# Two-layer hybrid encoder on one core: the start, the splitting of weights, two product ends and the last residual rewritten

## The chip, the core and the metric

The kernel runs on one core of a Trainium2 chip. The time is device microseconds of one execution; lower is better. The engines are TensorE (PE; its weight loads are listed apart as PEld), VectorE (DVE), ScalarE (ACT), GpSimd (POOL), and SyncE (SP), which here issues nearly all DMA transfers.

## The reference, cut to what matters

```python
for l in range(2):                      # x is (1, 1024, 1024), all float32
    z = rmsnorm(x, g_pre_mix[l]) @ w_in[l]            # 1024 -> 256 | 512 | 128 | 128 | 256
    zf, zq, zk, zv, zm = split(z)
    y_f = real(fft2 over (sequence, 64 channels) of zf) @ w_fourier[l]   # 4 groups
    y_a = window attention (|i-j| <= 128, 8 q heads, 2 kv heads, RoPE, sink)
    km, vm = split(rmsnorm(mem, g_mem[l]) @ w_mem_kv[l])    # 256 memory rows, 256 + 256 columns
    y_m = softmax(zm @ km^T / 8) @ vm                       # 4 heads
    y = concat(rmsnorm of y_f, y_a, y_m, with g_grp[l]) @ w_out[l]
    x = x + rmsnorm(y, g_post_mix[l])
    gate, up = split(rmsnorm(x, g_pre_ffn[l]) @ w_ffn_in[l])     # 2 x 2816
    x = x + rmsnorm((silu(gate) * up) @ w_ffn_out[l], g_post_ffn[l])
return x
```

## The kernel before, in words

**Split products.** Every large matrix product takes its operands as a high part (rounded to float32r) and a low part, what is left over, and adds three matmuls per block: high by high, high by low, low by high. `split` makes the two parts of a block: ACT casts the high part and DVE, or POOL where it is named, subtracts it from the block for the low one. Weights are loaded into a raw buffer first. `raws` is a ring of raw buffers at slots 0, 2 and 4 of the arena `arena_f` (a slot is 256 float32 columns), so three loads can be under way at once. Where a gain belongs to the weights (`g`, one number per weight row), it is multiplied in while the parts are made.

**Weight loads that the change touches.** `load_w` (L372) loads blocks into a raw buffer, has POOL scale them with `scaled` (L369) if there is a gain, and splits them. `zf_load` (L547) uses it for the 256 columns of w_in that give zT, with the low part on POOL. `load_w512` (L391) loads the eight 128x512 blocks of the kvz and q weights: in even blocks ACT writes the scaled high part and DVE makes the low part from the raw block in one instruction (L407); in odd blocks POOL scales the raw block in place, ACT casts and POOL subtracts. `Memory.load_k` loads the key half of w_mem_kv as two times 128 columns.

**The start.** Tiles of x (128 rows each) are loaded by `start_load`, squared and summed on ACT (`token_scale`), transposed on PE into PSUM banks of the pool "pd" and split into hT (`norm_T`). `fourier_tables` loads w_fourier and makes small tables with PE ("abp"). `prep` makes the position tables. `mem.make` loads the memory rows and weights, transposes the rows ("mTp") and makes keys and values ("kmp", "vmp", in "pd" banks as well). `mix.zf(half)` makes zT for four tiles out of hT and the zT weights, 48 matmuls of 512 columns, and then the products "pq" with the Fourier tables. Program order at the start is: tile 0, the pre-mix gains, tiles 1 to 3, the zT weights, tile 4; then the four tiles, the tables, `prep`, the memory, and last tiles 4 to 7 interleaved with `zf(0)`.

**The second feed-forward product.** `ffn_out` forms the 1024x1024 result from seven products of half-size blocks, in the order 5, 3, 4, 1, 7, 2, 6. Each has eleven steps k, and each step three matmuls into each of four PSUM banks p: 132 matmuls named "fo" (L1357). `out_sums` prepares a step: it loads a block of activations and one or two of weights, adds the two weight blocks on DVE (L1338) and splits both. The prepared operands of a step stand in a ring `abs_`, of six places in layer 0 and fifteen in layer 1. Products 3 and 7 go on adding in the PSUM banks of 5 and 1, so a bank has to be read out in between: after product 5 by two ACT copies per bank (L1381, L1382), after product 1 by a DVE addition (L1390). In layer 0 the work for layer 1 is put between: `mem.make` after product 3, `zf_load` and `fourier_tables` after product 1. In layer 1 the last tiles' output follows product 6, whose last two banks are done one after the other.

**The end.** `residual_out` squares and sums f (1024 columns) on ACT, makes 1/rms on POOL (two small instructions), then for each half of 512 columns multiplies f by it and by the gain (L354), adds it to x (L355, on POOL for tiles 1 and 3) and stores the half (L356).

**What sets the order.** The kernel is built with a planner (`schedule_with_timeline_sim=True`): it takes the program order as priorities, simulates a timeline with its own costs and from that writes out one fixed order of instructions for every engine and for SP. On the chip each engine goes through its order and waits where an operand is missing; whatever stands behind the waiting instruction on the same engine waits too. An edit at one place can therefore change the order at others. `tc.issue_after(ins)` holds the instructions of a block behind `ins`.

Of the kernel before, what the change touches and what calls it, by code (L numbers as in the profile page):

```python
# [19 lines left out]
P = 128  # L20
# [49 lines left out]
def tile_encoder(ctx: ExitStack, tc: tile.TileContext, T, C, out):  # L70
# [276 lines left out]
    def residual_out(x, f, g, dst, t):  # L347

        ss = sm(1, "rss")
        nc.scalar.activation(junks(D // 2).bitcast(BF16), f, AF.Square, accum_out=ss)  # L350
        r = rsqrt_mean(ss, D, 1, "rrs")
        for n in range(2):
            ns = slice(n * 512, n * 512 + 512)
            nc.vector.scalar_tensor_tensor(out=f[:, ns], in0=f[:, ns], scalar=r[:, 0:1], in1=g[:, ns], op0=ALU.mult, op1=ALU.mult)  # L354
            (nc.gpsimd if t in (1, 3) else nc.vector).tensor_tensor(out=x[:, ns], in0=x[:, ns], in1=f[:, ns], op=ALU.add)  # L355
            (nc.sync, nc.scalar)[n].dma_start(dst[:, ns], x[:, ns])  # L356
# [33 lines left out]

    def load_w512(w, c0, g):  # L391


        res = []
        for k in range(NK):
            if k % 2 == 0:
                t = big(2, 2, 512)
            raw = raws(512)
            nc.sync.dma_start(raw, w[k * P : k * P + P, c0 : c0 + 512])
            hi, lo = t[:, k % 2, 0], t[:, k % 2, 1]  # L400
            if k % 2:
                scaled(raw, g, k)
                split(hi, lo, raw, nc.gpsimd)
            else:
                gk = g[:, k : k + 1]
                nc.scalar.activation(hi, raw, AF.Copy, scale=gk)
                nc.vector.scalar_tensor_tensor(out=lo, in0=raw, scalar=gk, in1=f32(hi), op0=ALU.mult, op1=ALU.subtract)  # L407
            res.append((hi, lo))
        return res
# [31 lines left out]
    class Memory:  # L441
# [7 lines left out]
        def load_k(self):  # L449
            self.wk = [load_w(self.w, ci * P, P, self.kw + 8 * ci) for ci in range(2)]  # L450

        def load_v(self):
            self.wv = load_w(self.w, MW, MW, self.kw + 16)

        def rows(self):
            self.h = [at(self.kx + 4 + 4 * mt, D) for mt in range(2)]
            for mt in range(2):
                nc.sync.dma_start(self.h[mt], T["mem"][0, mt * P : (mt + 1) * P, :])

        def norm(self, mt):  # L460
            if mt == 0:
                self.g = gain(T["g_mem"][self.l], at(self.kx, D))
                self.mT = [[at(self.kt + 8 * i + 4 * kg, 4, NMEM, dt=F32R) for kg in range(2)] for i in range(2)]
            h = self.h[mt]
            norm_x(h, self.g)
            for kg in range(2):
                pt = ps([4, P], "mTp", "pT")
                for j in range(4):
                    k = kg * 4 + j
                    nc.tensor.transpose(pt[:, j, :], h[:, k * P : (k + 1) * P], ident)  # L470
                sl = slice(mt * P, mt * P + P)
                split(self.mT[0][kg][:, :, sl], self.mT[1][kg][:, :, sl], pt)
# [4 lines left out]
        def keys(self, ci):  # L477
            pt = ps([NMEM], "kmp", self.tag)
            acc = Acc(pt, NK)
            for k in range(NK):  # L480
                acc.add(self.wk[ci][k][0], self.wk[ci][k][1], self.m(0, k), self.m(1, k))
            nc.scalar.activation(at(self.ks + ci, NMEM), pt, AF.Copy, scale=QK_SCALE)
# [9 lines left out]
        def make(self):  # L492
            self.rows()
            self.load_k()
# [25 lines left out]
    class Mix:  # L520
# [26 lines left out]
        def zf_load(self):  # L547
            self.wzf = load_w(self.win, 0, 256, 64, nc.gpsimd, self.g)

# [164 lines left out]
        def kvz_load(self):  # L714

            self.wkvz = load_w512(self.win, FW + AW, self.g)
            self.vst, self.zst, self.kvr = {}, {}, {}
# [44 lines left out]
        def q_load(self):  # L762
            self.wq = load_w512(self.win, FW, self.g)
            self.qst, self.qr = {}, {}
# [577 lines left out]
    def ffn_out(l, actd, load, out, after, half, late):  # L1342
# [16 lines left out]
        for i in (5, 3, 4, 1, 7, 2, 6):  # L1359
# [5 lines left out]
            for k in range(n):  # L1365
                ops.append(out_sums(l, actd, i, k))
                for p in range(whole):
                    step(pts[p], p, ops[k], k == 0, k == n - 1, new)
# [6 lines left out]
            for p in range(4):  # L1375
                pt = pts[p]
                if p >= whole:
                    for k in range(n):
                        step(pt, p, ops[k], k == 0, k == n - 1, new)
                if i == 5:  # L1380
                    nc.scalar.copy(c22[p], pt)  # L1381
                    nc.scalar.copy(c11[p], pt)  # L1382
                if i == 3:
                    nc.scalar.copy(c12[p], pt)
                    TT(out=c22[p], in0=pt, in1=c22[p], op=sub)
                if i == 4:
# [45 lines left out]
    mix = Mix(0, hT, mem)  # L1432
    start_load(0)
    gains_T(gpT, T["g_pre_mix"], at(15, P))
    for t in range(1, 4):
        start_load(t)
    mix.zf_load()
    start_load(4)
# [4 lines left out]
    mem.make()  # L1443
    weave([lambda t=t: start_tile(t) for t in range(4, 8)], [lambda: mix.zf(0)])

    for l in range(DEPTH):
        mix.zf(1, 2)
        mix.kvz_load()
        kvz = mix.skewed(mix.kvz, mix.kvz_turn, NT)
        weave(mix.fourier_units(), kvz[:8] + [mix.q_load] + kvz[8:])  # L1450
# [143 lines left out]
```

## Time and profile before

| | |
|---|---|
| median of 3 runs | 2010.85 us (2010.7 to 2011.73) |
| the profiled execution | 2013.01 us, its span 2011.2 us |
| mean granted clock of PE | 0.995 |
| busy PE, PEld | 1967.6 us (98%), 1628.7 us (81%) |
| busy DVE, ACT, POOL | 1489.6, 1047.6, 657.2 us (74%, 52%, 33%) |
| moved by DMA | 288.56 MB, 143 GB/s over the span |

The rows of the profile name an instruction by the line of the kernel that issues it, often a line of a helper (L176 and L177 are the two lines of `split`), by engine and operation, and by the tiles it writes and reads. In the view of waits a row gives who waited, for whom, how long in sum, how often and the longest. In the order of time a row gives start, duration, instruction and count, and in brackets the idle time before it with what ended it. The granted clock is a share of TensorE's full clock.

### The profile page before, as it was taken

How to read it: one execution, taken by the hardware profiler on the slowest of the kernel's cores; microseconds unless marked ns; L12 is line 12 of the kernel's file. 1: busy time of each engine (PE TensorE's matmuls, PEld its weight loads, DVE VectorE, ACT ScalarE, POOL GpSimd, SP SyncE). 2: the span in 40 equal slices, each digit the busy share in tenths (PEclk: the TensorE clock that was granted, in tenths of full speed). 3: DMA queues.
4: the chain of work that ended last, by engine and by line, in shares of the span. 5: the costliest groups of instructions: out<-in, count | busy, mean ns of one | idle time of the engine just before them, and what ended most of it. 6: DMA issues, size and time to landing. Idle time of an engine off the chain costs nothing.

```text
span 2011.2 us, 28323 instructions
## 1 busy us (share of the span) xinstructions
PE 1967.6 (98%) x9587; PEld 1628.7 (81%) x9587; DVE 1489.6 (74%) x2364; ACT 1047.6 (52%) x2204; POOL 657.2 (33%) x793
## 2 busy tenths in 40 slices
PE   8999999999999999999999999999999999999998
PEld 7877888788888888887888778877888888887886
DVE  5566867888777766678866677679887777778776
ACT  6476877643433334554555678676343333345541
POOL 4345445204334333002423654451134333400021
PEclk9999999999999999999999999999999999999999
DMA  6210323444323224979831113244332332379973
GB/s 214 64 59 27 110 101 127 135 131 136 100 95 121 85 88 157 310 265 322 286 132 45 53 59 116 95 147 126 126 120 95 121 100 95 110 232 330 314 273 116
DMA packets 181889, 288.56 MB, mean 143 GB/s; under 512 B 15560, under 2 KB 81648, under 8 KB 181744
## 3 DMA queue, kind: packets, MB, share of 16 engines
q1 hardware_dynamic: 173680, 267.88, 40.1%
q10 hardware_dynamic: 8064, 18.88, 2.4%
q8 instruction: 75, 1.23, 0.3%
q14 instruction: 70, 0.57, 0.1%
HBM read 220.11 MB, written 66.58 MB: 143 GB/s over the span
## 4 chain that ended last, share of the span: by engine, by line
PE 87%; DVE 3%; DMA 3%; ACT 2%; issue 2%; POOL 2%; SPq 0%; DVEq 0%; POOLq 0%; ACTq 0%
PE fo L1357 18%; PE qy L1193 12%; PE qx L1193 12%; PE qc L1193 11%; PE mo L187 7%; PE qz L1193 6%; PE kvp L187 4%; PE qp L187 4%; PE zT L187 2%; PE sc L793 2%; PE pT L831 2%; PE qa L1193 1%; PE av L844 1%; DMA arena_f<-in_w_ffn_out 1%; DVE arena_r L177 1%
## 5 line engine op out<-in xcount | busy, mean ns | idle before, releaser
L1357 PE MATMUL fo<-arena_r 128*128 128x512 f32 x1512 | 354.6, 391 | 6.6 <-ACT big L1382 4.0
L1357 PEld LDWEIGHTS fo<-arena_r 128*128 128x128 f32 x1512 | 284.0, 188 | 66.2 <-ACT big L1382 4.8
L176 ACT CAST arena_r<-arena_f 128x512 fp32r<-128x512 f32 (+2 forms) x344 | 185.8, 572 | 179.5 <-DMA arena_f<-actd 69.2
L177 DVE TENSOR_TENSOR arena_r<-arena_f,arena_r 128x512 fp32r<-128x512 f32 x262 | 182.3, 727 | 52.0 <-ACT arena_r L176 44.2
L1193 PE MATMUL qc<-arena_r,flex 128*128 128x512 f32 x912 | 220.8, 390 | 0.0
L1183 ACT CAST flex<-arena_f 128x512 fp32r<-128x512 f32 x148 | 91.8, 621 | 232.2 <-PE qy L1193 71.3
L1193 PEld LDWEIGHTS qc<-arena_r,flex 128*128 128x128 f32 x912 | 171.1, 188 | 37.1 <-DVE flex L1125 0.2
L1193 PE MATMUL qy<-arena_r,flex 128*128 128x512 f32 x576 | 139.4, 389 | 0.0
L1183 ACT CAST arena_r<-arena_f 128x512 fp32r<-128x512 f32 x92 | 57.0, 621 | 156.6 <-DVE arena_f L1180 63.7
L1193 PEld LDWEIGHTS qy<-arena_r,flex 128*128 128x128 f32 x576 | 108.0, 188 | 22.6
L1184 DVE TENSOR_TENSOR flex<-arena_f,flex 128x512 fp32r<-128x512 f32 x148 | 108.4, 734 | 22.7 <-ACT flex L1183 22.7
L1227 POOL TENSOR_TENSOR arena_f<-arena_f 128x512 f32<-128x512 f32 x36 | 48.1, 1336 | 231.7 <-ACT arena_f L1198 231.7
L1193 PE MATMUL qx<-arena_r 128*128 128x512 f32 x360 | 119.5, 389 | 0.0
L1193 PE MATMUL qy<-arena_r 128*128 128x512 f32 x480 | 116.4, 389 | 0.0
L1184 DVE TENSOR_TENSOR arena_r<-arena_f,arena_r 128x512 fp32r<-128x512 f32 x92 | 67.7, 736 | 62.6 <-ACT arena_r L1183 60.5
L1193 PE MATMUL qz<-arena_r,flex 128*128 128x512 f32 x320 | 106.8, 395 | 0.0
L1259 POOL TENSOR_TENSOR arena_f<-arena_f,flex 128x512 f32<-128x512 f32 x28 | 45.7, 1632 | 184.9 <-DVE arena_f L1230 114.1
L1193 PEld LDWEIGHTS qy<-arena_r 128*128 128x128 f32 x480 | 90.1, 188 | 18.7
L1234 POOL TENSOR_TENSOR arena_f<-arena_f 128x512 f32<-128x512 f32 x36 | 60.0, 1668 | 126.5 <-DVE arena_f L1233 126.5
L187 PE MATMUL mo<-big,arena_r 128*128 128x512 f32 x384 | 100.4, 398 | 0.5 <-ACT arena_f L1043 0.5
L1193 PE MATMUL qx<-flex,flex 128*128 128x512 f32 x304 | 100.1, 390 | 0.0
L1180 DVE TENSOR_TENSOR arena_f<-arena_f 128x512 f32<-128x512 f32 x90 | 92.5, 1033 | 4.4 <-DMA arena_f<-in_w_ffn_in 2.9
(315 smaller groups left out, 4624.1 us busy)
## 6 DMA issues: line engine op xcount, KB each, us to landing
arena_f<-in_w_ffn_out SPq DMA_DIRECT2D x264, 256.0 KB, 4.7
actd<-arena_f SPq DMA_DIRECT2D x154, 256.0 KB, 3.0
arena_f<-actd SPq DMA_DIRECT2D x154, 256.0 KB, 4.5
arena_f<-in_w_ffn_in SPq DMA_DIRECT2D x46, 512.0 KB, 3.9
big<-in_w_ffn_in SPq DMA_DIRECT2D x40, 512.0 KB, 4.5
arena_f<-in_w_in SPq DMA_DIRECT2D x40, 256.0 KB, 2.9
arena_f<-in_x SPq DMA_DIRECT2D x16, 512.0 KB, 5.3
arena_f<-in_w_out SPq DMA_DIRECT2D x32, 256.0 KB, 2.7
```

The lines of the kernel that those rows point to most:

```text
L176: nc.scalar.copy(hi, src)
L177: return (lo_eng or nc.vector).tensor_tensor(out=lo, in0=src, in1=f32(hi), op=ALU.subtract)
L187: mm(self.dst, a, b, start=self.i == 0, stop=self.i == self.n - 1)
L793: mm(pt, lhs, self.kst[g][i][:, k0 * P : k1 * P], start=i == 0, stop=i == 1)
L1180: nc.vector.tensor_tensor(out=s, in0=x, in1=y, op=op)
L1183: self.cast = nc.scalar.copy(w[:, 0], s)
L1184: self.lo = nc.vector.tensor_tensor(out=w[:, 1], in0=s, in1=f32(w[:, 0]), op=ALU.subtract)
L1193: mm(pt, a, b, start=start and n == 0, stop=n == 11, skip_group_check=not start)
L1227: G(out=self.u2, in0=self.u2, in1=self.p1, op=ALU.add)
L1234: G(out=self.p5, in0=self.p1, in1=self.p5, op=ALU.add)
L1259: (G if i % 2 else nc.vector).tensor_tensor(out=q.act[i], in0=c, in1=g[i], op=ALU.mult)
L1357: mm(pt, ab[:, 0, x, sl], ab[:, 1, y], start=new and first and j == 0, stop=last and j == 2, skip_group_check=not new)
```

## The change

Several edits are made together.

- `residual_out` works by halves: ACT squares each half with a sum of its own, POOL adds the sums, DVE multiplies f by the gain meanwhile, and one DVE instruction scales and adds to x.
- `zf_load` no longer uses `load_w`: POOL writes the scaled high part from the raw block and DVE makes the low part from the raw block. `load_w512` does the same for the odd blocks of layer 1's kvz weights; layer 0's kvz and both layers' q weights stay as they were (`early`).
- `load_k` loads 256 columns at once; `keys` slices them.
- Start: seven raw buffers until `kvz_load`; the zT weights ahead of tiles 2 and 3; memory rows and their gain right behind tile 3; zT of the first half in two passes (`zf(0, 2)`).
- `ffn_out`: in products 5 and 1 the last three steps are done bank by bank; after product 5 one copy (c11) is made instead of two, and product 3 subtracts that one.

```diff
     def residual_out(x, f, g, dst, t):
+        ss, v, r = (sm(2, "rss2"), sm(2, "rrsv2"), sm(1, "rrs"))
+        cols = [slice(n * 512, n * 512 + 512) for n in range(2)]
+        for n, ns in enumerate(cols):
+            nc.scalar.activation(junks(256).bitcast(BF16), f[:, ns], AF.Square, accum_out=ss[:, n : n + 1])
+            nc.gpsimd.tensor_scalar(
+                out=v[:, n : n + 1], in0=ss[:, n : n + 1], scalar1=1.0 / D, scalar2=v[:, 0:1] if n else EPS, op0=ALU.mult, op1=ALU.add
+            )
+            nc.vector.tensor_tensor(out=f[:, ns], in0=f[:, ns], in1=g[:, ns], op=ALU.mult)
+        nc.gpsimd.tensor_tensor(out=r, in0=v[:, 1:2], in1=mhalf[:, 0:1], op=ALU.pow)
+        for n, ns in enumerate(cols):
+            nc.vector.scalar_tensor_tensor(out=x[:, ns], in0=f[:, ns], scalar=r[:, 0:1], in1=x[:, ns], op0=ALU.mult, op1=ALU.add)
             (nc.sync, nc.scalar)[n].dma_start(dst[:, ns], x[:, ns])
...
-    def load_w512(w, c0, g):
+    def load_w512(w, c0, g, early):
...
-            if k % 2:
+            gk = g[:, k : k + 1]
+            if k % 2 and early:
                 scaled(raw, g, k)
                 split(hi, lo, raw, nc.gpsimd)
+                res.append((hi, lo))
+                continue
+            if k % 2:
+                nc.gpsimd.tensor_scalar(out=hi, in0=raw, scalar1=gk, scalar2=1.0, op0=ALU.mult, op1=ALU.mult)
             else:
-                gk = g[:, k : k + 1]
                 nc.scalar.activation(hi, raw, AF.Copy, scale=gk)
-                nc.vector.scalar_tensor_tensor(out=lo, in0=raw, scalar=gk, in1=f32(hi), op0=ALU.mult, op1=ALU.subtract)
+            nc.vector.scalar_tensor_tensor(out=lo, in0=raw, scalar=gk, in1=f32(hi), op0=ALU.mult, op1=ALU.subtract)
...
         def load_k(self):
-            self.wk = [load_w(self.w, ci * P, P, self.kw + 8 * ci) for ci in range(2)]
+            self.wk = load_w(self.w, 0, MW, self.kw)
...
         def zf_load(self):
-            self.wzf = load_w(self.win, 0, 256, 64, nc.gpsimd, self.g)
+            self.wzf = []
+            for k0 in (0, 4):
+                hi, lo = at(64 + 2 * k0, 4, 256, dt=F32R), at(68 + 2 * k0, 4, 256, dt=F32R)
+                for j in (0, 2):
+                    raw = raws(2, 256)
...
+                        nc.gpsimd.tensor_scalar(out=h, in0=raw[:, i], scalar1=g, scalar2=1.0, op0=ALU.mult, op1=ALU.mult)
+                        nc.vector.scalar_tensor_tensor(
+                            out=lo[:, j + i], in0=raw[:, i], scalar=g, in1=f32(h), op0=ALU.mult, op1=ALU.subtract
+                        )
...
-                for p in range(whole):
+                for p in range(whole if i not in (5, 1) or k < n - 3 else 0):
                     step(pts[p], p, ops[k], k == 0, k == n - 1, new)
...
-                if p >= whole:
-                    for k in range(n):
-                        step(pt, p, ops[k], k == 0, k == n - 1, new)
+                for k in range(0 if p >= whole else n - 3 if i in (5, 1) else n, n):
+                    step(pt, p, ops[k], k == 0, k == n - 1, new)
                 if i == 5:
-                    nc.scalar.copy(c22[p], pt)
                     nc.scalar.copy(c11[p], pt)
                 if i == 3:
                     nc.scalar.copy(c12[p], pt)
-                    TT(out=c22[p], in0=pt, in1=c22[p], op=sub)
+                    TT(out=c22[p], in0=pt, in1=c11[p], op=sub)
...
     start_load(0)
+    raws.ks = (0, 2, 4, 52, 54, 44, 46)
     gains_T(gpT, T["g_pre_mix"], at(15, P))
-    for t in range(1, 4):
+    start_load(1)
+    mix.zf_load()
+    for t in range(2, 4):
         start_load(t)
-    mix.zf_load()
+    mem.rows()
     start_load(4)
...
-    weave([lambda t=t: start_tile(t) for t in range(4, 8)], [lambda: mix.zf(0)])
+    weave([lambda t=t: start_tile(t) for t in range(4, 8)], [lambda: mix.zf(0, 2)])
...
         mix.kvz_load()
+        raws.ks, raws.i = (0, 2, 4), 0
```

More of the change, by code (lines that the diff above doesn't have):

```diff
@@ L347, in residual_out @@
     def residual_out(x, f, g, dst, t):
[L349 to L355, printed above, removed]
+        ss, v, r = (sm(2, "rss2"), sm(2, "rrsv2"), sm(1, "rrs"))
[9 more added lines that the diff above has]
+            nc.vector.scalar_tensor_tensor(out=x[:, ns], in0=f[:, ns], scalar=r[:, 0:1], in1=x[:, ns], op0=ALU.mult, op1=ALU.add)
             (nc.sync, nc.scalar)[n].dma_start(dst[:, ns], x[:, ns])
@@ L455, in rows @@
         def rows(self):
+            self.g = gain(T["g_mem"][self.l], at(self.kx, D))
             self.h = [at(self.kx + 4 + 4 * mt, D) for mt in range(2)]
@@ L461, in norm @@
             if mt == 0:
-                self.g = gain(T["g_mem"][self.l], at(self.kx, D))
                 self.mT = [[at(self.kt + 8 * i + 4 * kg, 4, NMEM, dt=F32R) for kg in range(2)] for i in range(2)]
@@ L479, in keys @@
             acc = Acc(pt, NK)
+            cs = slice(ci * P, ci * P + P)
             for k in range(NK):
-                acc.add(self.wk[ci][k][0], self.wk[ci][k][1], self.m(0, k), self.m(1, k))
+                acc.add(self.wk[k][0][:, cs], self.wk[k][1][:, cs], self.m(0, k), self.m(1, k))
             nc.scalar.activation(at(self.ks + ci, NMEM), pt, AF.Copy, scale=QK_SCALE)
@@ L492, in make @@
         def make(self):
-            self.rows()
+            if self.l:
+                self.rows()
             self.load_k()
@@ L547, in zf_load @@
         def zf_load(self):
-            self.wzf = load_w(self.win, 0, 256, 64, nc.gpsimd, self.g)
+            self.wzf = []
[3 more added lines that the diff above has]
+                    raw = raws(2, 256)
+                    r0 = (k0 + j) * P
+                    nc.sync.dma_start(raw, self.win[r0 : r0 + 2 * P, 0:256].rearrange("(k p) c -> p k c", p=P))
+                    for i in range(2):
+                        g = self.g[:, k0 + j + i : k0 + j + i + 1]
+                        h = hi[:, j + i]
+                        nc.gpsimd.tensor_scalar(out=h, in0=raw[:, i], scalar1=g, scalar2=1.0, op0=ALU.mult, op1=ALU.mult)
+                        nc.vector.scalar_tensor_tensor(
+                            out=lo[:, j + i], in0=raw[:, i], scalar=g, in1=f32(h), op0=ALU.mult, op1=ALU.subtract
+                        )
+                self.wzf += [(hi[:, i], lo[:, i]) for i in range(4)]
         def zf(self, half, parts=1):
@@ L714, in kvz_load @@
         def kvz_load(self):
-            self.wkvz = load_w512(self.win, FW + AW, self.g)
+            self.wkvz = load_w512(self.win, FW + AW, self.g, self.l == 0)
             self.vst, self.zst, self.kvr = {}, {}, {}
@@ L762, in q_load @@
         def q_load(self):
-            self.wq = load_w512(self.win, FW, self.g)
+            self.wq = load_w512(self.win, FW, self.g, True)
             self.qst, self.qr = {}, {}
```

## The prediction

> **What bounds the kernel now.** I read the page first, then who TensorE waited for, then its busy time in short stretches, and at each wait found there the order of time.
>
> ```profile
> PE 1967.6 (98%) x9587; PEld 1628.7 (81%) x9587; DVE 1489.6 (74%) x2364; ACT 1047.6 (52%) x2204; POOL 657.2 (33%) x793
> ...
> PE ggp L248 <- DMA flex<-in_g_pre_mix: 4.6, 1, 4.6
> PE fo L1357 <- ACT big L1382: 4.0, 2, 3.5
> PE zT L187 <- ACT flex L176: 3.6, 1, 3.6
> PE abp L538 <- DMA arena_f<-in_w_fourier: 2.7, 1, 2.7
> PE fo L1357 <- ACT arena_r L176: 2.6, 1, 2.6
> ...
> PE zT L187 <- ACT arena_r L176: 1.7, 1, 1.7
> ```
>
> TensorE is busy 1967.6 of 2011.2 us, so no edit off its path pays. What can be won is the 43.6 us in which it is idle, and the stretches in which it is busy but slow. Six waits hold 19.2 us of the idle time: four in the first 60 us (4.6, 3.6, 2.7, 1.7), two (4.0 and 2.6) inside the second feed-forward product. The 4.6 is the first load, which no edit moves. The end of the span adds one more block, below. Columns of the next rows: stretch, its length, busy time and count of PE, PEld, DVE, ACT, POOL, granted clock, DMA share, GB/s.
>
> ```profile
> 10.00:15.00 5.00, 2.33 (x12) 2.20 (x12) 2.52 (x5) 4.70 (x12) 4.53 (x10) 1.00 1.00 331
> 20.00:25.00 5.00, 5.00 (x16) 4.00 (x17) 2.94 (x4) 4.35 (x11) 4.33 (x8) 1.00 0.88 295
> 50.00:55.00 5.00, 1.35 (x11) 1.11 (x10) 1.54 (x3) 3.65 (x8) 4.50 (x5) 0.92 0.65 206
> 55.00:60.00 5.00, 5.00 (x34) 5.00 (x33) 2.90 (x4) 3.15 (x6) 1.35 (x2) 0.74 0.28 90
> 900.00:940.00 40.00, 37.40 (x169) 30.98 (x167) 35.01 (x53) 18.88 (x37) 13.11 (x13) 1.00 0.95 325
> 1815.00:1820.00 5.00, 1.59 (x8) 0.97 (x6) 3.87 (x7) 2.19 (x6) 0.00 (x0) 0.88 0.97 327
> 1820.00:1825.00 5.00, 4.91 (x12) 3.84 (x13) 3.50 (x6) 5.00 (x12) 0.00 (x0) 0.50 1.00 359
> ```
>
> Early on ACT and POOL, not TensorE, are full (4.70 and 4.53 of 5). After two idle blocks, the ones at 50 and at 1816, the granted clock is down to 0.74 and 0.50.
>
> **Edit 1, `residual_out`, the end.**
>
> ```profile
> 2002.56 0.69 DVE L1397 TENSOR_TENSOR big<-fo,big 128x512 f32<-128x512 f32 x1 [1.98 <-PE fo L1357]
> 2003.35 1.06 ACT L350 ACTIVATE arena_f<-big 128x1024 bf16<-128x1024 f32 x1 [6.33 <-DVE big L1397]
> ...
> 2004.86 0.55 POOL L237 TENSOR_TENSOR rrs<-rrsv,const 128x1 f32<-128x1 f32 x1
> 2005.44 1.42 DVE L354 SCALAR_TENSOR_TENSOR big<-big,rrs,flex 128x512 f32<-128x512 f32 x2 [2.19 <-POOL rrs L237]
> 2006.77 1.29 DVE L355 TENSOR_TENSOR arena_f<-arena_f,big 128x512 f32<-128x512 f32 x2
> 2008.09 0.34 ACTq L356 DMA_DIRECT2D out<-arena_f  x1
> ```
>
> After the last product nothing covers these rows. In the last tile only the right half of f changes in the last product, so the left half's Square and its multiplication by g go under matmuls. What stays: Square of 512 columns, an estimate of 0.58 (a 512-wide ACT copy, below) for 1.06, saves 0.48; the two additions (1.29) vanish because the last instruction adds while it scales, saves 1.29; the multiplication by g (0.69) runs on DVE while ACT and POOL make r. The last store leaves at about 2006.3 instead of 2008.09: 1.75 us less (bounds 1.2, if the halved Square costs the full 1.06, and 2.0). The other tiles' tails, with the additions that POOL made for tiles 1 and 3 now on DVE, stand beside matmuls: nothing; uncovered they would cost a few tenths each.
>
> **Edit 2, the staggered end of products 5 and 1, and one copy instead of two.** Layer 1, product 5 into 3:
>
> ```profile
> 1808.23 0.69 DVE L177 TENSOR_TENSOR arena_r<-arena_f,arena_r 128x512 fp32r<-128x512 f32 x1
> ...
> 1813.71 2.88 PE L1357 MATMUL fo<-arena_r 128*128 128x512 f32 x12
> ...
> 1818.45 0.62 ACT L176 CAST arena_r<-arena_f 128x512 fp32r<-128x512 f32 x1 [1.07 <-DVE arena_f L1338]
> 1818.97 0.58 ACT L1381 COPY big<-fo 128x512 f32<-128x512 f32 x1
> 1819.45 0.59 ACT L1382 COPY big<-fo 128x512 f32<-128x512 f32 x1
> ...
> 1820.09 1.65 PE L1357 MATMUL fo<-arena_r 128*128 128x512 f32 x3 [3.50 <-ACT big L1382]
> ...
> 1825.38 1.69 PE L1357 MATMUL fo<-arena_r 128*128 128x512 f32 x6
> ```
>
> Product 5 ends at 1816.59. Its copies stand on ACT behind a cast that waits for a DVE sum, the sum for a load; the first product-3 matmul may not add to the PSUM bank until it is copied, so 3.50 us are idle. Then 12 matmuls take 1820.09 to 1825.38, 5.29 us, where the twelve at 1813.71 start 0.226 us apart (2.88 less 0.39 over 11): 2.7 us, so 2.6 more are lost at the half clock. The change lets bank 0 finish 27 matmuls early (27 x 0.226 = 6.1 us), bank 1 4.1, bank 2 2.0; each needs one 0.58 copy. Bank 3 ends with the product and is asked for 9 matmuls (2.0 us) later; if its copy is again behind a waiting cast I leave 0.6 us. Gain 3.5 + 2.6 - 0.6 = 5.5 (bounds 0 and 6.1).
>
> Against it: blocks 8 to 10 of the product must be ready earlier, block 10 at 1816.59 - 6.8 = 1809.8 instead of 1813.71. Its low part ends by 1808.9 (the first row), so it fits, by 0.9 us. In layer 0 the same wait is 4.0 - 3.5 = 0.5: gain 0.5. Three operand buffers are held longer, of six in layer 0; blocks 3 to 5 of the next product start their casts up to 4 us later, while they are needed 8 us after the product's end: nothing, but if that lead were missing, up to 4 us each at the two ends in layer 0.
>
> [...]
>
> Layer 0, product 1 into 7:
>
> ```profile
> 928.87 2.35 DVE L177 TENSOR_TENSOR arena_r<-arena_f,arena_r 128x512 fp32r<-128x512 f32 x2
> 929.03 1.64 POOL L177 TENSOR_TENSOR arena_r<-arena_f,arena_r 128x512 fp32r<-128x512 f32 x1 [1.22 <-ACT arena_r L176]
> 931.15 0.68 DVE L1338 TENSOR_TENSOR arena_f<-arena_f 128x512 f32<-128x512 f32 x1
> ...
> 931.75 0.68 DVE L1390 TENSOR_TENSOR big<-fo,big 128x512 f32<-128x512 f32 x1
> ...
> 932.57 1.61 PE L1357 MATMUL fo<-arena_r 128*128 128x512 f32 x6 [2.60 <-ACT arena_r L176]
> ```
>
> The wait is put down to ACT, but bank 0's addition on DVE (L1390) ends at 932.43, just ahead of PE; I take that as the cause: it is queued behind three DVE instructions, two of them slow (2.35 for 1.4) beside POOL's subtraction. Bank 0 now ends 6.1 us earlier: gain 2.6, less 0.6 left over: 2.0 (bounds -2 and 2.6, since DVE is 35.01 of 40 busy here).
>
> **Edit 3, POOL writes the high part, DVE makes the low one (`zf_load`, and layer 1's odd kvz blocks).**
>
> ```profile
> L177 POOL TENSOR_TENSOR arena_r<-arena_f,arena_r 128x512 fp32r<-128x512 f32 x4 | 5.1, 1274 | 0.0
> L369 POOL TENSOR_SCALAR arena_f<-arena_f,const 128x256 f32<-128x256 f32 (+1 forms) x9 | 4.7, 532 | 13.9 <-DVE flex L288 13.8
> ...
> L288 DVE SCALAR_TENSOR_TENSOR flex<-flex 128x256 f32<-128x256 f32 x10 | 4.6, 458 | 0.1
> ```
>
> Per `zf_load`: POOL loses four subtractions, 5.1 us, ACT four casts (4 x 0.62 = 2.5), POOL keeps eight scalings of about 0.5, DVE gains 8 x 0.458 = 3.7. At the start that is a relief, since ACT and POOL are full and DVE at 2.52 of 5. In layer 0's product 1 it lands on the busy DVE, but takes away the POOL subtraction that stretched DVE; I set the two against each other. A new wait: DVE now waits for POOL, and POOL for the weights' load; behind it stand L1338 and L1390, for which PE waits. Layer 1's kvz: four DVE instructions of some 0.75 beside matmuls: nothing, 3 us if that cover were gone. `load_k` loads four 256 KB blocks before and after, and `keys` only slices them: nothing. Layer 0's kvz weights come through seven raw buffers instead of three, beside matmuls: nothing.
>
> **Edit 4, the start.**
>
> ```profile
> 18.33 18.88 SPq L383 DMA_DIRECT2D arena_f<-in_w_mem_kv  x8
> ...
> 19.83 4.47 PE L187 MATMUL zT<-arena_r 128*128 128x512 f32 x11
> ...
> 43.08 1.58 PE L187 MATMUL vmp<-arena_r 128*128 128x256 f32 x12
> ```
>
> The memory weights' eight loads take 18.33 to 37.2 us because three raw buffers take turns; their products hold the "pd" PSUM banks for which the transposes of x tiles 4 and up wait; these come late, and so the 3.6 at 51. Seven buffers end that: gain 3.6, and the slow clock behind it (34 matmuls against some 45 in the next 5 us, 11 of 0.11): 1.2. The zT weights are loaded ahead of x2 and x3, and zT's first half-column pass needs only tiles 0 and 1, so TensorE has work at about 11 us instead of 17.6. Of the 2.7 + 1.7 idle and the half-speed stretch (11 zT in 4.47 us where 2.5 would do, 2.0 lost) I take half, 3.2. Against it: 96 halves at 0.118 for 48 whole at 0.226, 0.5 more; x2 and x3 land 1 MB / 331 GB/s = 3 us later. In sum 3.6 + 1.2 + 3.2 - 0.5 = 7.5 (bounds -6, if w_fourier lands 6.8 later as in the first rival and nothing is won back, and 12, if nearly all the idle time and the slow clock go).
>
> **The sum.** 1.75 + 5.5 + 0.5 + 2.0 + 7.5 = 17.2. The planner orders every queue anew; for one or two fresh waits like the 1.7 above I add 2.2. The profiled execution took 2013.0 us (span 2011.2): 1998.0. The median of the runs shown, 2010.85, is 2.2 below it: 1996.
>
> **The rivals.**
> - The start gives nothing. For: TensorE's queue is in order, and 2.7 us of it already waited for w_fourier at 12.8 us. If the fourth w_in block, g_mem and mem and x4 (0.25 + 1.5 + 0.5 = 2.25 MB) get ahead of it on SP, it lands 6.8 us later. Against: the planner may keep it early. 1996 + 7.5 = 2003.5.
> - The waits in the products move: blocks 8 to 10 late, or copies still behind waiting casts. For: the spare time of 0.9 us. Against: the sums of product 3 were already being made at 1811. 1996 + 8 = 2004. One mechanism that would do part of it: DVE's new instruction reads the raw block and the high part while POOL scales the next block, and the row at 928.87 shows two DVE instructions with two inputs at 2.35 for 1.4 beside a POOL one. With eight such meetings of 0.5 us DVE is 4 us later at product 1's end, and the 2.0 turn into -2: 2000. [...]
> - Slower: the same w_fourier wait, but with transposes, zT and the memory products all queued behind it on TensorE. Each us that it lands after 19 us is lost in full, with half clock behind. The other edits save 9.7 - 2.2 = 7.5; it decides from a loss of 7.5 at the start, w_fourier at some 27 us; at 32 us the time is about 2016.
> - The start gives its whole bound: 1991.
>
> **Chances.** Forecast 0.55 (own range 1991 to 2001), start gives nothing 0.18, waits move 0.14, whole start 0.07, slower 0.06. The range of 8 in 10 takes in the first, third and part of the second: 1987 to 2007. A measurement of this kernel tells 0.2%, 4 us, from no change: under 2006.8 is faster. The two middle rivals stay below it for the most part; of each I give a quarter to no change. Faster 0.85, same 0.09, slower 0.06.
>
> **What would show it.** Right: last store some 6 us behind the last matmul's start instead of 7; no wait at the product 5 into 3 of layer 1 over 1 us and a clock of 1.00 there; the 2.6 at 930 under 1; memory loads done by 28 us and no clock of 0.74 at the start. Wrong: abp waiting more than 2.7 us, a wait inside the last three blocks of product 5 or 1, DVE idle on POOL between 905 and 940.

## The result, and the profile after

| | before | after |
|---|---|---|
| median of 6 runs each | 2011.07 us (2007.76 to 2015.37) | 1999.16 us (1996.99 to 2002.84) |
| ratio, 95% interval | | 0.994 (0.9926 to 0.9955) |
| the profiled execution | 2013.01 us, span 2011.2 | 2000.0 us, span 1998.2 |
| mean granted clock of PE | 0.995 | 0.997 |

The kernel is 0.6% faster, by 9 to 15 us. The forecast was 1996, with a range of 1987 to 2007. The page of after, its engine totals, and who TensorE waited for (us in sum, times, longest):

```profile
PE 1967.0 (98%) x9635; PEld 1629.2 (82%) x9635; DVE 1499.4 (75%) x2390; ACT 1040.1 (52%) x2202; POOL 642.7 (32%) x785
...
PE ggp L248 <- DMA flex<-in_g_pre_mix: 4.7, 1, 4.7
PE qa L1217 <- ACT flex L1207: 2.0, 4, 0.5
PE zT L187 <- DVE arena_r L177: 1.8, 1, 1.8
PE mpT L957 <- POOL arena_f L947: 1.2, 3, 0.6
PE hTp L1142 <- DVE arena_f L321: 1.2, 1, 1.2
```

TensorE is busy as long as before (1967.0 against 1967.6). Its idle time fell from 43.6 to 31.2 us; these 12.4 are nearly all of the 13.0 by which the span fell. Five of the six waits that the prediction counted are no longer in the list at their length: only the first load's 4.7 stands. The stretches that answer to those shown of before (length, busy time and count of PE, PEld, DVE, ACT, POOL, granted clock, DMA share, GB/s):

```profile
10.00:15.00 5.00, 3.66 (x17) 3.66 (x18) 3.98 (x8) 3.49 (x7) 4.49 (x11) 1.00 1.04 407
...
20.00:25.00 5.00, 4.06 (x35) 3.92 (x34) 3.38 (x8) 4.22 (x12) 1.35 (x4) 1.00 0.90 257
...
30.00:35.00 5.00, 3.14 (x23) 2.50 (x22) 4.97 (x13) 4.97 (x12) 1.69 (x3) 1.00 0.72 220
...
50.00:55.00 5.00, 3.80 (x27) 3.26 (x28) 2.06 (x4) 4.31 (x10) 1.13 (x4) 1.00 0.26 105
55.00:60.00 5.00, 5.00 (x45) 5.00 (x44) 2.92 (x5) 1.92 (x4) 0.00 (x0) 1.00 0.01 3
900.00:940.00 40.00, 40.00 (x181) 33.21 (x181) 37.48 (x68) 18.93 (x39) 7.21 (x8) 1.00 0.99 344
...
1810.00:1815.00 5.00, 5.00 (x23) 4.13 (x22) 4.57 (x8) 4.40 (x9) 0.00 (x0) 1.00 0.92 309
```

Read them against the earlier rows. POOL is as full as before at 10 to 15 (4.49 of 5 for 4.53), but at 20 to 25, where it was at 4.33, it is at 1.35. At 30 to 35 DVE and ACT are now the full ones (4.97 each). At 50 to 60 TensorE's clock stays at 1.00. The stretch 900 to 940 has no idle time left, though DVE is busier (37.48 for 35.01), and the two stretches at half clock in the layer-1 product are gone.

Layer 1, product 5 into 3, in order of time:

```profile
1807.84 0.57 ACT L1404 COPY big<-fo 128x512 f32<-128x512 f32 x1
1809.53 0.62 ACT L176 CAST arena_r<-arena_f 128x512 fp32r<-128x512 f32 x1 [1.12 <-DVE arena_f L1362]
1810.06 0.58 ACT L1404 COPY big<-fo 128x512 f32<-128x512 f32 x1
...
1811.06 0.59 ACT L1404 COPY big<-fo 128x512 f32<-128x512 f32 x1
```

A cast still waits 1.12 us for a DVE sum, with a copy behind it. But the copies are one per bank and the banks finish one after the other, so no matmul waits. Layer 0, product 1 into 7:

```profile
924.05 1.09 DVE L569 SCALAR_TENSOR_TENSOR arena_r<-arena_f,const,arena_r 128x256 fp32r<-128x256 f32 x2 [0.39 <-POOL arena_r L568]
925.06 1.27 DVE L1412 TENSOR_TENSOR big<-fo,big 128x512 f32<-128x512 f32 x2
...
926.86 0.68 DVE L1412 TENSOR_TENSOR big<-fo,big 128x512 f32<-128x512 f32 x1
```

DVE does wait for POOL (0.39), but the additions that free the PSUM banks (L1412) come at their undisturbed length (1.27 for two). The end:

```profile
1990.65 0.69 DVE L1419 TENSOR_TENSOR big<-fo,big 128x512 f32<-128x512 f32 x1 [2.63 <-PE fo L1381]
1991.44 0.63 ACT L352 ACTIVATE arena_f<-big 128x512 bf16<-128x512 f32 x1 [6.00 <-DVE big L1419]
...
1992.33 0.68 POOL L353 TENSOR_SCALAR rrsv<-rss,rrsv 128x1 f32<-128x1 f32 x1 [4.92 <-ACT arena_f L352]
1993.10 0.55 POOL L357 TENSOR_TENSOR rrs<-rrsv,const 128x1 f32<-128x1 f32 x1
1993.68 1.42 DVE L359 SCALAR_TENSOR_TENSOR arena_f<-big,rrs,arena_f 128x512 f32<-128x512 f32 x2 [0.80 <-POOL rrs L357]
...
1995.13 0.34 ACTq L360 DMA_DIRECT2D out<-arena_f  x1
```

From the last addition to the last store it is 4.48 us for 5.53 before: 1.05 less. To see where the rest went I took, for each product, the start of its last matmul in a stage (view by tile; the last two times of a row are the first and last start). Layer 0's q product and the mixer's output product, before and then after:

```profile
L187 PE MATMUL qp<-big,flex x48: 387/393/481, 155.5 to 192.0; 128*128 128x512 f32 x48
...
L187 PE MATMUL mo<-flex,arena_r x96: 387/390/482, 283.7 to 370.6; 128*128 128x512 f32 x96
```

```profile
L187 PE MATMUL qp<-big,flex x48: 387/393/481, 151.1 to 187.7; 128*128 128x512 f32 x48
...
L187 PE MATMUL mo<-flex,arena_r x96: 387/390/628, 280.3 to 368.8; 128*128 128x512 f32 x96
```

So after is 4.3 us ahead at 190 and only 1.8 ahead at 370. The whole way by the same markers:

| stage, from marker to marker | before | after | difference |
|---|---|---|---|
| start to last layer-0 q matmul | 192.0 | 187.7 | -4.3 |
| to last mixer output matmul | 178.6 | 181.1 | +2.5 |
| first feed-forward product, layer 0 | 424.8 | 424.8 | 0 |
| to the last layer-1 memory product (holds layer 0's 5 into 3) | 86.3 | 85.5 | -0.8 |
| to layer 1's first zT (holds 1 into 7) | 151.6 | 148.5 | -3.1 |
| layer 1's zT, kvz and q | 147.2 | 146.0 | -1.2 |
| layer 1 to last mixer output, and its first feed-forward product | 605.8 | 607.2 | +1.4 |
| layer 1's second feed-forward product (holds 5 into 3) | 215.8 | 209.4 | -6.4 |
| last matmul to the end of the span | 9.1 | 8.0 | -1.1 |

The sum is -13.0. These are two single executions; the runs of one kernel spread over some us (before, in one set of 26: 2006.1 to 2019.1), so a difference below about 2 us counts only where a row shows its cause. The second and the sixth row need care: over all thirteen traces of this document the stage to the last mixer output takes 178.6 to 181.5 us and layer 1's zT, kvz and q 144.7 to 147.2, and before has the shortest of the one and the longest of the other. Below, "the markers" are these.

### The profile page after: what moved, and what is told of

Same layout as the page of the kernel before. It is cut to its first block, busy times and chain, and to the rows that moved or that the text cites. A ratio compares the mean times of both kernels' runs of the same rounds, so it can differ in the third digit from the quotient of the medians.

```text
span 1998.2 us, 28454 instructions
## 1 busy us (share of the span) xinstructions
PE 1967.0 (98%) x9635; PEld 1629.2 (82%) x9635; DVE 1499.4 (75%) x2390; ACT 1040.1 (52%) x2202; POOL 642.7 (32%) x785
## 4 chain that ended last, share of the span: by engine, by line
PE 90%; DVE 3%; ACT 2%; issue 2%; POOL 2%; DMA 1%; DVEq 0%; POOLq 0%; SPq 0%; ACTq 0%
PE fo L1381 20%; PE qx L1217 12%; PE qy L1217 12%; PE qc L1217 11%; PE mo L187 8%; PE qz L1217 6%; PE kvp L187 4%; PE qp L187 3%; PE sc L817 2%; PE pT L855 2%; PE zT L187 2%; PE av L868 1%; PE qa L1217 1%; PE ssp L1024 1%; PE av L871 1%
## 5 line engine op out<-in xcount | busy, mean ns | idle before, releaser
L176 ACT CAST arena_r<-arena_f 128x512 fp32r<-128x512 f32 (+2 forms) x336 | 180.6, 569 | 167.7 <-DMA arena_f<-actd 75.1
L177 DVE TENSOR_TENSOR arena_r<-arena_f,arena_r 128x512 fp32r<-128x512 f32 x262 | 177.2, 709 | 39.3 <-ACT arena_r L176 29.8
L1208 DVE TENSOR_TENSOR arena_r<-arena_f,arena_r 128x512 fp32r<-128x512 f32 x92 | 66.8, 726 | 63.0 <-ACT arena_r L1207 60.5
```

The source lines that it names most:

```text
L176: nc.scalar.copy(hi, src)
L177: return (lo_eng or nc.vector).tensor_tensor(out=lo, in0=src, in1=f32(hi), op=ALU.subtract)
L1208: self.lo = nc.vector.tensor_tensor(out=w[:, 1], in0=s, in1=f32(w[:, 0]), op=ALU.subtract)
```

## The experiments

Six kernels do one part of the change, half of one, or two parts, on top of before; five undo, extend or shift one part of after. Those given with a ratio were timed in rounds against before on the same chip; three (three raw buffers, one copy, one pass) were run once.

**1. The tail alone** (before, with the new `residual_out`).

> The kernel before with the new residual_out alone. Between the two profiles the time from the last matmul's end to the end of the span fell from 8.7 to 7.6 us, 1.1 where 1.75 was forecast. If the edits simply add up: 7.6 us here too, the rest as before, ratio to before 0.9994, not to be told from 1. Rival: the planner's order shifts elsewhere, and the span differs from before by more than 3 us away from the end.

Measured: 2009.44 us, ratio 0.9986 (0.9972 to 0.9999). Its end, from last matmul to the end of the span, is 8.0 us for 9.1. But the planner's order of the layer-1 product changed as well. The wait of product 5 into 3, and the stretch behind it:

```profile
PE fo L1361 <- ACT big L1386: 2.6, 1, 2.6
...
1820.00:1825.00 5.00, 5.00 (x24) 4.14 (x23) 5.00 (x10) 3.92 (x8) 0.00 (x0) 1.00 0.88 310
```

2.6 instead of 3.5, and behind it 24 matmuls at clock 1.00 where before had 12 at 0.50. That product takes 212.3 us for 215.8. An edit of 1.1 us thus shows as 6.9 us in the span of this one execution, and by the ratio as 2.8 in the times (0.2 to 5.6). The tail's own part is the 1.1.

**2. The split between POOL and DVE alone** (before, with the new `zf_load` and `load_w512`).

> The kernel before with POOL writing the high part and DVE the low part (zT weights, layer 1's odd kvz blocks) alone. Theory: it buys little by itself: the wait of 2.6 us between product 1 and 7 in layer 0 stays within 1.5 of that since bank 0's addition still comes late, the start gains 0 to 2 us; ratio 0.998 to 1.001. Rival: POOL's subtraction beside DVE was the cause of the 2.6, then it is under 0.5 here with no staggering, and the start gains 4 us or more; ratio 0.996 or less.

Measured: 2017.04 us, ratio 1.002 (1.0006 to 1.0035): slower.

```profile
PE fo L1375 <- ACT big L1400: 5.0, 2, 3.3
PE qa L1211 <- ACT flex L1201: 3.2, 3, 1.8
...
PE fo L1375 <- ACT arena_r L176: 0.4, 1, 0.4
```

The last row is product 1 into 7: 0.4 for 2.6, without any staggered end. In order of time, the two DVE subtractions ahead of bank 0's addition:

```profile
932.84 1.28 DVE L177 TENSOR_TENSOR arena_r<-arena_f,arena_r 128x512 fp32r<-128x512 f32 x2
```

1.28 us, where the same two took 2.35 in before beside POOL's subtraction. A little earlier in before two others took 3.21, and one addition 1.78 instead of 0.68, also beside POOL. With all that away 2.2 of the 2.6 is gone. What it loses is elsewhere: the start gains nothing (last layer-0 q matmul 192.7), product 5 into 3 of layer 0 waits 1.7 for 0.5, and the first feed-forward product of layer 1 takes 427.3 us for 424.9.

**3. The feed-forward edits alone** (before, with the staggered ends and one copy).

> The kernel before with the staggered ends of products 5 and 1 and the single copy alone. Theory: it carries the 6.4 us of layer 1's product 5 into 3 (3.5 idle, about 2.7 at half clock), 0.5 in layer 0, and the 2.6 in layer 0's product 1 into 7: 9.5 us, ratio 0.9953. Rival: the 2.6 went with the POOL subtraction: then the wait there stays over 1.5, and the gain is 7 us, 0.9965.

Measured: 2006.03 us, ratio 0.9967 (0.9954 to 0.998). The layer-1 product takes 209.4 us, as in after, and of all waits for product banks one is left:

```profile
PE fo L1357 <- DVE big L1388: 0.5, 1, 0.5
```

So either this edit or experiment 2's removes most of the 2.6, and they don't add there; the 5 into 3 of layer 1 is this edit's.

**4. The start alone** (before, with the seven raw buffers, the new order of loads, `load_k` and two passes of zT).

> The kernel before with the start edits alone (order of loads, seven raw buffers, two passes of zT, 256 columns in load_k), the zT weights still split by ACT and POOL. In the two profiles the last q product of layer 0 starts 4.3 us earlier, 7.5 was forecast at the start. Theory: order and buffers carry it, the last qp matmul starts 3 to 5 us earlier than the 192.0 of before; ratio 0.998. Rival: it needs the split, since ACT and POOL were full: then under 2 us here, ratio 0.999 to 1.

Measured: 2011.39 us, ratio 0.9998 (0.9985 to 1.0012). The last layer-0 q matmul is at 191.6, 0.4 earlier than before.

```profile
PE zT L187 <- ACT arena_r L176: 1.7, 1, 1.7
...
10.00:15.00 5.00, 3.09 (x15) 2.65 (x16) 2.08 (x3) 4.78 (x10) 5.00 (x9) 0.72 1.04 414
15.00:20.00 5.00, 5.00 (x29) 5.00 (x29) 0.69 (x1) 3.25 (x7) 4.50 (x8) 0.60 1.05 383
```

The loads come earlier, but the engines that prepare the operands don't: POOL is busy 5.00 of 5 and ACT 4.78 at 10 to 15, while DVE has 2.08 and then 0.69. The rearranged loads reach a full POOL.

**5. Start and split together** (before, with both).

> The kernel before with the start edits and the POOL/DVE split together, ffn_out and the end as before. Alone, the start edits had the last layer-0 qp matmul at 191.6 and the split at 192.7, before at 192.0, the whole change at 187.7. Theory: the two need each other (the early zT passes want operands that ACT and POOL could not make in time), so the last qp matmul starts at 187 to 189 here. Rival: the 4.3 us in the whole change came by chance of the planner's order with the other edits; then 191 to 193. The wait in layer 1's product 5 into 3 stays at about 3.5 us with the half clock.

Measured: 2002.9 us, ratio 0.9957 (0.994 to 0.9974). The last layer-0 q matmul is at 188.8. The one part gains nothing, the other loses, and together they are 3.2 us ahead at that marker. Chance of the order is an unlikely cause: the four kernels without any edit to the start or to the split have the marker at 191.9 to 194.6, the three that have both, with nothing of the start taken back or moved (this one, after, and experiment 7, which extends the split), at 187.7 to 188.8. Its product 5 into 3 of layer 1 waited 1.5 instead of the expected 3.5, in a product of 211.3 us: the order of the queue had moved again. With that, its 8.6 us are not all the start's, and they don't add to the 6.6 of experiment 3 (after has 12). At product 1 into 7 a wait of 1.1 is left here, with the split and without the stagger.

**6. After with three raw buffers at the start** (run once).

> The changed kernel with three raw buffers at the start instead of seven. Theory of the prediction (the memory weights' loads were held by the three buffers, 3.6 + 1.2 us): the last qp matmul moves from 187.7 to 191 or later, and the wait of some 3 us before the second half of zT is back. Rival: the buffers do not matter, since ACT and DVE are full from 25 to 50 us in any case: 187 to 189.

```diff
     start_load(0)
-    raws.ks = (0, 2, 4, 52, 54, 44, 46)
     gains_T(gpT, T["g_pre_mix"], at(15, P))
```

Measured: 2007.46 us, span 2005.7, last layer-0 q matmul 195.5.

```profile
PE zT L187 <- ACT flex L176: 3.3, 1, 3.3
PE zT L187 <- POOL arena_r L568: 2.8, 1, 2.8
...
55.00:60.00 5.00, 4.89 (x28) 4.89 (x29) 2.07 (x3) 1.71 (x4) 0.00 (x0) 0.66 0.08 25
```

Both the wait of the start's second half (3.3) and the slow clock behind it (0.66) are back, and a new wait for POOL's scaling with them. The buffers are what the other parts of the start rest on: 7.8 us at this marker, more than the 4.8 that the theory gave them.

**7. After with the new split for layer 0's kvz too.**

> The changed kernel with layer 0's kvz weights split in the new way as well (POOL writes the high part, DVE the low). In the changed kernel DVE takes 9.2 us from 39.9 to 48.9 for work that takes 4.3 alone, beside four POOL subtractions of layer 0's kvz weights; ACT waits 2.2 us for it, and a key/value copy and the transposes of tile 4 wait behind. Theory: without those POOL subtractions DVE reaches its last table instruction 2 us or more earlier, the wait of 1.1 us at 50 goes, and the last qp matmul starts at 184.5 to 186.5; ratio to before 0.9925 to 0.994. Rival: DVE is simply full there and three more us of work make it worse: 188 to 191.

```diff
-            self.wkvz = load_w512(self.win, FW + AW, self.g, self.l == 0)
+            self.wkvz = load_w512(self.win, FW + AW, self.g, False)
```

Measured: 2000.37 us, ratio 0.9941 (0.9921 to 0.9961): the same as after. The last layer-0 q matmul is at 188.8, 1.1 later than in after and not earlier: the theory failed, and the rival's range holds. What it was to relieve, in after (POOL's subtractions for these weights, and DVE's rotary tables):

```profile
44.74 2.88 POOL L177 TENSOR_TENSOR big<-arena_f,big 128x512 fp32r<-128x512 f32 x2
...
43.88 4.95 DVE L288 SCALAR_TENSOR_TENSOR flex<-flex 128x256 f32<-128x256 f32 x6
```

and in experiment 7:

```profile
45.62 2.72 DVE L288 SCALAR_TENSOR_TENSOR flex<-flex 128x256 f32<-128x256 f32 x6
...
PE zT L187 <- ACT flex L176: 2.8, 1, 2.8
```

Six instructions take 4.95 us beside POOL's subtractions and 2.72 without them. But DVE gets four instructions of 0.75 in exchange, so its chain of tables ends at 48.3 us instead of 48.8, and a zT waits 2.8 for a cast of ACT. The work that came to DVE takes up what the tables won.

**8. One copy without the staggered ends** (before; run once).

> The kernel before with one copy per bank after product 5 instead of two, and no staggering. Before, the stretch from the last qz to the last fo matmul of layer 1 was 215.8 us, with staggering and one copy 209.4. Theory: the wait is for the first copy, which stands behind casts that wait for loads, so one copy fewer does not move it: wait 2.5 to 3.5 us, stretch 212 to 216. Rival: the second copies were the load on ACT: wait under 1, stretch under 211.

```diff
                 if i == 5:
-                    nc.scalar.copy(c22[p], pt)
                     nc.scalar.copy(c11[p], pt)
...
-                    TT(out=c22[p], in0=pt, in1=c22[p], op=sub)
+                    TT(out=c22[p], in0=pt, in1=c11[p], op=sub)
```

Measured: 2017.67 us, span 2015.9 (before in the same set: 2007.7 to 2016.0).

```profile
1824.63 0.62 ACT L176 CAST arena_r<-arena_f 128x512 fp32r<-128x512 f32 x1 [1.26 <-DVE arena_f L1338]
1825.16 0.58 ACT L1380 COPY big<-fo 128x512 f32<-128x512 f32 x1
1825.79 1.65 PE L1357 MATMUL fo<-arena_r 128*128 128x512 f32 x3 [2.30 <-ACT big L1380]
```

With one copy the wait is 2.3 us instead of 3.5, of which the second copy is some 0.5; the rest of the difference is that the first copy starts sooner behind the product (1.67 us for 2.38). What is left is the waiting cast ahead of the first copy. It takes the stagger to get rid of it. The three matmuls behind the wait take 1.65 us, as the three behind the 3.50 of before: half clock here too:

```profile
1825.79:1829.10 3.31, 3.31 (x8) 2.64 (x9) 3.00 (x6) 3.25 (x7) 0.00 (x0) 0.50 1.05 369
```

The stretch that the theory put at 212 to 216 takes 213.6. That the whole is slower than most runs of before comes from elsewhere: the last layer-0 q matmul is at 194.6 for 192.0, and the stage to layer 1's first zT takes 154.3 for 151.6.

**9. After with zT's first half in one pass** (run once).

> The changed kernel with the first half of zT in one pass of 512 columns instead of two of 256. Theory: the two passes give TensorE its work before tiles 2 and 3 are there; without them the first zT matmul starts at 14 us or later instead of 8.8, and the last qp matmul at 189 to 192 instead of 187.7. Rival: later waits set the pace at the start (DVE and ACT full from 25 to 50), then the last qp matmul stays within 1 us of 187.7.

```diff
-    weave([lambda t=t: start_tile(t) for t in range(4, 8)], [lambda: mix.zf(0, 2)])
+    weave([lambda t=t: start_tile(t) for t in range(4, 8)], [lambda: mix.zf(0)])
```

Measured: 2011.44 us, span 2009.6, last layer-0 q matmul 197.5.

```profile
15.36 11.16 PE L187 MATMUL zT<-arena_r 128*128 128x512 f32 x42 [1.33 <-POOL nrsv L235]
...
42.57 2.71 PE L187 MATMUL kmp<-arena_r,flex 128*128 128x256 f32 x11 [4.14 <-DVE arena_r L177]
```

The first zT starts at 15.4 us instead of 8.8, and the memory's product then waits 4.1 us for its operands. Behind that wait eleven of its matmuls take 2.71 us, where the eleven at 45.29 us take 1.61. All this comes to 9.8 us at this marker, more than the 1.3 to 4.3 of the theory and than the 7.8 of the buffers.

**10 and 11. After with `prep()`, the rotary tables and sinks, behind the memory's products** (10), and so with experiment 7's split as well (11). In after DVE is full at 30 to 50 us, partly with these tables.

```diff
-    prep()
     mem.make()
+    prep()
```

> The changed kernel with the position tables (prep) behind the memory part in program order. They are some 10 us of DVE between 30 and 50 us, and ACT's Sin holds the copy of the values behind it. Theory: the tables hold up the memory part and tile 4's transposes; moved behind, the last vmp matmul starts 2 us or more before 47.5 and the last qp matmul at 184 to 187; ratio to before 0.992 to 0.994. Rival: the tables are wanted by the first rope soon after, so the wait only moves to kvz: last qp matmul at 187 to 190.

> The same with layer 0's kvz weights split in the new way too. Alone that took the stretch out of the table instructions (6 in 2.72 us instead of 4.95) but filled DVE with four more, and the last qp matmul started 1.1 us later. Theory: with the tables out of the way the four fit, last qp matmul 1 us or more ahead of the run with the tables late alone, ratio 0.991 to 0.9935. Rival: DVE stays the limit to 50 us, no better than the run with the tables late alone.

Measured: 2003.92 us, ratio 0.9965 (0.9951 to 0.9978), and 2003.79 us, ratio 0.9961 (0.9946 to 0.9976): both behind after by the median (1999.16), though the intervals overlap a little with that of after (0.9926 to 0.9955). Of experiment 10:

```profile
PE qa L1217 <- ACT flex L1207: 3.7, 3, 2.7
...
PE ms L936 <- ACT flex L433: 1.8, 1, 1.8
PE ms L936 <- DVE flex L437: 1.5, 1, 1.5
```

The last layer-0 memory product starts 1.1 us earlier (46.4), but the last q matmul is at 191.2, against 187.7 in after: before the memory scores ("ms") TensorE now waits 3.3 us for casts of ACT and low parts of DVE, where after doesn't wait at all. That the tables put behind made these late isn't shown. The theory of 184 to 187 failed for 10, and 190.9 in 11 is no real gain on it. And the first feed-forward product of layer 0 takes some 428 us instead of 424.8, with a new wait of 2.7. No version tried here beats after.

## Why the prediction came out as it did

The sign was right and the size near: 1999.2 measured, 1996 predicted. Of the places, those in the feed-forward products were right; the start gave little more than half of its term. That the total comes this close is in part luck: against the terms below, the start, the tail and the fresh waits are 5.6 us short together, and the product ends and layer 1's zT, kvz and q 3.5 us over. The terms, on the profiled executions:

| term | forecast | found | by |
|---|---|---|---|
| tail | -1.75 | -1.1 | rows of the end, experiment 1 |
| layer 1, 5 into 3 | -5.5 | -6.4 | markers, experiment 3 |
| layer 0, 5 into 3 | -0.5 | -0.8 | markers |
| layer 0, 1 into 7 | -2.0 | -3.1 | markers, experiments 2 and 3 |
| start | -7.5 | -4.3 | markers, experiments 4 to 6 and 9 |
| layer 1's zT, kvz, q | 0 | -1.2 | markers |
| fresh waits | +2.2 | +2.5, and +1.4 in layer 1 | markers |

**The start was the mis-sized term.** The step that failed is "Seven buffers end that: gain 3.6". The buffers are needed (experiment 6) and the memory loads are all issued by 28.15 us, as the prediction asked. The 3.6 us wait and the clock of 0.74 are gone. But the last memory product moved from 48.7 to 47.5 only, by 1.2 us, and not by the nine that the loads gained. The working had looked at the loads and the PSUM banks, not at the engines that split the loaded blocks: DVE and ACT are at 4.97 of 5 at 30 to 35 us, DVE at 4.96 up to 45.

So other waits came where the old ones went: in the first 60 us the 3.6, 2.7 and 1.7 are gone, 8.0 in all, and waits of 0.2 to 1.8 us for ACT and DVE, 6.5 in all, stand in after. The first zT of the second half starts at 52.51 us instead of 54.66: 2.15 us of the 4.3, where the prediction had 3.6 + 3.2 - 0.5 = 6.3. The other 2.15 come behind it: 1.0 less idle time up to the marker, and 1.1 in the speed, for which the prediction had 1.2 ("the slow clock behind it"); that part held.

Experiment 7 shows what fills DVE: nearly half of its time on those six table instructions goes with POOL's subtractions beside them (4.95 us, and 2.72 without them), and the edit that takes those away gives DVE the work instead. The second part, half "Of the 2.7 + 1.7 idle and the half-speed stretch", fell short too. The 2.7 for w_fourier is gone, but the zT waits of the first half are 1.8 and 1.2 in sum, so 1.4 of 4.4 us is won. And:

```profile
11.34 4.21 PE L187 MATMUL zT<-arena_r 128*128 128x256 f32 x18 [1.80 <-DVE arena_r L177]
```

18 half-width matmuls in 4.21 us are 0.23 each, twice the 0.118 of the prediction. That stretch is still at half speed, though the granted clock of its stretch reads 1.00. The reason is in the record, not in the chip: the trace of after has no clock record ahead of 17.4 us (before: 23.4), and the column counts time without a record as full clock. From 17.56 us on, 24 such matmuls take 3.11 us, 0.13 each. In experiment 4 the same stretch reads 0.72 and 0.60, and the twelve at 13.35 us take 2.93. Ahead of the first record the spacing of the matmuls is what tells the speed.

**The split set at zero was wrong in both directions.** The prediction set its two effects against each other. Alone it costs 0.2% (experiment 2). With the start's edits it makes the difference between 0.4 us and 3.2 of the start's 4.3 (experiments 4 and 5). It is a relief for POOL, and that pays only where POOL's output is what comes last. It also takes most of the 2.6 at 1 into 7 by itself: with neither the split nor the stagger this wait is 1.7 to 2.9 us (before and experiments 1, 4 and 8), with the split alone 0.4 and 1.1 (experiments 2 and 5). That bears out the cause given for it (bank 0's addition behind DVE instructions stretched by POOL); but the split also takes casts off ACT, and no run here separates the two. The stagger removes the same wait in another way (experiment 3).

**The layer-1 product was right**, wait and slow clock together. The order of the queues moved this wait too, but only within 1.5 to 3.7 us in the six kernels without the stagger; in the seven with it there is none. The 0.6 that I left for a copy behind a waiting cast wasn't needed. No matmul waited for blocks 8 to 10: the lead of 0.9 us was enough.

**The tail was short by 0.7.** Square and its accumulation saved 0.34 (forecast 0.48), the last DVE instructions 1.20 (forecast 1.29). The step that failed is that a longer first small instruction on POOL was costed at nothing. Before, it took a constant as its second operand; now that operand is a column of one number per row:

```profile
2004.58 0.19 POOL L235 TENSOR_SCALAR rrsv<-rss 128x1 f32<-128x1 f32 x1 [6.65 <-ACT arena_f L350]
```

0.19 us became 0.68: 0.49 lost. 0.34 + 1.20 - 0.49 = 1.05. The sign "some 6 us behind the last matmul's start instead of 7" had the level wrong: the last store was already 5.96 us behind it before, and is 4.90 behind it in after.

**The fresh waits** came larger than allowed for, 3.9 us for 2.2 (2.7 with the 1.2 won in layer 1's zT, kvz and q set against them), and where they fell was not foreseen. Between 190 and 370 us after loses 2.5. One piece is a wait of 1.1 for ACT (the scores, L817 on L959) that before did not have. Another is a slow clock around 360; before, then after:

```profile
360.00:365.00 5.00, 3.78 (x28) 2.70 (x26) 5.00 (x7) 2.90 (x8) 3.17 (x4) 1.00 0.65 213
```

```profile
360.00:365.00 5.00, 4.39 (x20) 3.74 (x21) 5.00 (x10) 3.12 (x7) 2.04 (x4) 0.71 0.57 166
```

Both have the same 1.2 us wait near there (L1142 and L1118 for L321). Why the clock drops in the one and not in the other is open. Part of the 2.5 is that before is the fastest of the thirteen kernels in this stage.

**The rivals.** "The start gives nothing" is what experiment 4 does, so it was a near thing, but for another reason than the one given: no kernel with the start's edits waited for w_fourier; ACT and POOL were late (zT waits of 1.7 and 1.2 in experiment 4). "The waits in the products move" didn't happen in after; the mechanism under it, DVE slower beside POOL, is seen in after too (4.95 us, for 2.72 in experiment 7), only at 44 us, and no longer at 925. The slower rival needed a late w_fourier and fell with it. Of the signs of being wrong one did show: DVE idle on POOL between 905 and 940, 0.8 us in two waits. No matmul waited for it.

**The half clock.** In before and after, up to the end of the matmuls, half clock comes in stretches of 3.41 us or two times that (before: 54.15 to 57.57, 1125.94 to 1129.35, 1818.85 to 1825.67; after: 362.11 to 365.52, 1184.72 to 1188.13). Their starts lie on a grid: those of before are 314 and 203 times 3.413 us apart, those of after 241 times. Below, a window is one step of this grid.

In the window ahead of the half clock TensorE was idle for 2.26 us in before (the wait of 3.50, the rest of which lies in the next window). The wait of 2.60 at 930 in before falls on two windows, 1.40 and 1.19; the clock stays at 1.00. In these two traces, from the first clock record up to 1985 us, a window at full clock with more than 1.7 us idle was followed by half clock each time (3.14, 2.26 and 1.74, all in before), one with 1.00 or less never. In between both occur: 1.13 and 1.23 were followed by it in after, and 1.13, 1.47 and 1.49 there and 1.19 to 1.40 in before were not. What decides between them isn't shown. Elsewhere half clock followed waits of 3.29 (experiment 2) and 2.30 (experiment 8), and none followed the 2.55 of experiment 1 (1.00 from 1810 to 1825). The loss behind 3.50 us is 2.6 because half clock lasted two windows, with twelve matmuls at 5.29 us (5.28 in experiment 2, behind 3.29). The drop near 360 us in after follows a window with 1.23 us idle; before has one with 1.22 and no drop.

## What to carry to other kernels

Before costing an earlier load, look at which engine turns the loaded block into an operand: in experiment 4 that engine was full (POOL, 5.00 of 5), and the earlier loads gained 0.4 us at the last layer-0 q matmul. Here the relief of such an engine and the earlier load paid only together (3.2 in experiment 5). A PSUM bank that must be read between two accumulations should end staggered from its neighbours where its reader sits in a queue behind casts that wait for something else: of the 3.50 us here 2.30 were left with one copy alone (experiment 8), and none with the stagger. A wait of TensorE of some 2 us is worth more than itself if half clock follows, as behind the 2.30 of experiment 8 (3.31 us at 0.50). In a kernel whose order a planner writes, a part tried alone tells its own rows (the end, one wait), and its total carries some us of other order changes; compare stage by stage.

## What was not expected of the hardware

- A DVE instruction with two SBUF inputs (128x256) takes 0.83 us beside POOL subtractions in after and 0.45 without them in experiment 7 (4.95 and 2.72 for six), a factor of 1.8. POOL's own take 1.44 to 1.51 there, and 1.27 at 14 us in before.
- POOL's 128x1 TENSOR_SCALAR with a column as second operand takes 0.68 us in the last tile of after, with a constant 0.19 in that of before. Both forms vary: over the eight tiles of after's last product the column form takes 0.45 to 1.16 us, the other 0.19 to 0.75.
- The matmuls at the start run at half speed: 0.23 us for 256 columns at 11 us in after (0.13 from 17.56 us on), 0.41 for 512 at 20 us in before (0.226 at 1813.71). They do so also where the granted clock, for want of a record, reads 1.00.
- In before and after half clock begins and ends on a grid of 3.413 us. 1.23 us idle in one step of it was followed by half clock in after, and 1.49 elsewhere in after wasn't.
